# A decoder block on one core: operands of the second norm made in stages and carried into the gate projection's first group

## The chip, the cores and the metric

The kernel runs on one core of a Trainium2 chip. The metric is the device time of one execution in microseconds. TensorE does the matrix products, VectorE and ScalarE the element-wise work that may read PSUM, GpSimd element-wise work in SBUF only, and SyncE starts the transfers.

## The reference

One layer of a hybrid decoder trunk on 512 tokens with 2048 channels, in float32:

```python
h = _rms_norm(x, norm1_g[l])
proj = h @ w_in[l]
...
mix = jnp.concatenate([out_a.astype(x.dtype), out_b.astype(x.dtype),
                       out_c.astype(x.dtype)], axis=-1)
x = x + mix @ w_out[l]
h2 = _rms_norm(x, norm2_g[l])
x = x + (jax.nn.silu(h2 @ w_gate[l]) * (h2 @ w_up[l])) @ w_down[l]
```

Here out_a is a dilated attention of 8 heads, out_b a convolution module of 512 channels and out_c a windowed attention of 16 heads; mix has 2048 columns. The feed-forward part has 5632 hidden channels (44 tiles of 128).

## The kernel before

Activations are kept transposed: a tile is 128 channels by 512 tokens. Every product is made of a high and a low part: a float32 operand is copied to a rounded format (ScalarE) and the remainder is the low part (VectorE, a subtraction). All instructions stand in the order in which the program issues them; each engine works through its own queue in that order.

**The output projection** runs in two halves over the rows of mix: ROWS[0:8] and ROWS[8:16]. In each half, 16 units (one weight tile of 128 x 1024 for one output tile n, in the order OUT_ORDER[half]) take 8 x 3 matmuls each. In the first half the output is added to x (L830); in the second it is added again (L833), which gives x2, and x2 is stored to DRAM, squared and summed into ssum2 for norm 2 (L344 to L348). split_mix (L739, L740) splits a row of mix; split_rows calls it for the next three rows ahead of a matmul. Rows a0 to a3 are split as soon as their attention is done; rows b0 to b3 wait in mix until the second half asks for them. Rows b come from the convolution.

**Ticks** are a schedule written by hand: ticks.after(n, f) runs f at the n-th next tick, ticks.drain() runs all that is due. Each output unit has two ticks, in its middle and at its end. A residual stands due at the tick in the middle of the unit after its own. After two units of the second half everything due is drained and PSUM is reopened as 4 banks of products and 2 buffers called high (two banks each).

**The feed-forward products** use a seven-product scheme (Strassen's, in a variant) over halves of channels and tokens. For a pair of tiles j and j + 8 of x2, h2_of(j) scales both (L815), forms four differences of halves (L820 to L823: n1, n3, n2, n4), and splits seven 128 x 256 operands (helper operand, L808 on ScalarE and L809 on VectorE), numbered q = 5, 1, 7, 6, 2, 4, 3 in the order of use. ops[q, j] holds a high half and a low half side by side. Pair j is made when tile j + 8 has its residual.

Weights are split two units ahead: L226 and L227 while the output projection's layout of PSUM stands, then L230 (a copy into a high buffer), L231, and L232, whose second input is that copy in PSUM. Sums of weight blocks are made on GpSimd (L178) at set units.

**Gate's first group** (g = 0) has seven units, q = 5, 1, 7, 6, 2, 4, 3, each 8 + 8 matmuls at L924 over j = 0 to 7. The first two units take j = 0 to 5, then both take j = 6 and 7 (EARLY = 6). Between them stands norm 2: norm2a sums ssum2 over channels with TensorE (L289) and takes the power on GpSimd (L356), norm2b spreads the result over partitions by transposes (L295) and copies it out (L887, L888). Both use the bank outs[3], which unit 6 needs.

Of the kernel before, what the change touches and what calls it, by code (L numbers as in the profile page):

```python
# [15 lines left out]
P = 128  # L16
T = 512
# [11 lines left out]
TAPS = 31  # L29
NB = 4  # L30

OUT_ORDER = (list(range(16)), [n + o for n in range(8) for o in (0, 8)])
TAP_TICKS = 1.72


# [78 lines left out]
def kernel(ctx: ExitStack, tc: tile.TileContext, xT, wi, wo, wgu, wd, cst_in, outT):  # L114
# [19 lines left out]
    def slot(name, dt=F32, cols=T):  # L134
        return sp.tile([P, cols], dt, name=name, tag="s")
# [146 lines left out]
    def col(i):  # L282
        return cst[:, i:i + 1]
# [7 lines left out]
    def spread(src4, name, b=None):  # L291

        b = bank(name) if b is None else b
        for i in range(NT):
            nc.tensor.transpose(b[:, i * P:(i + 1) * P], src4[:, i:i + 1].to_broadcast([P, P]), ident)  # L295
        return b
# [45 lines left out]
    def add_square(acc, x, k, tag, eng=nc.gpsimd):  # L342
        if k == 0:
            nc.scalar.activation(acc, x, AF.Square)  # L344
        else:
            sq = slot(f"{tag}{k}")
            nc.scalar.activation(sq, x, AF.Square)  # L347
            eng.tensor_add(acc, acc, sq)  # L348

    def token_scale(acc, n, name, b=None):  # L350

        b = bank(name, NT) if b is None else b
        stat_rows(b[:, :, None], acc, ones)
        v, r = small(name + "v"), small(name + "r")
        nc.vector.tensor_scalar(v, b, 1.0 / n, EPS, op0=ALU.mult, op1=ALU.add)
        nc.gpsimd.tensor_tensor(r, v, nhalf[:, :NT], op=ALU.pow)  # L356
        return v, r
# [377 lines left out]
    def split_mix(name):  # L735
        if name not in m_hi:
            m = mix.pop(name)
            hi, lo = slot(f"mh_{name}", F32R), slot(f"ml_{name}", F32R)
            nc.scalar.copy(hi, m)  # L739
            nc.vector.tensor_sub(lo, m, hi.bitcast(F32))  # L740
            m_hi[name], m_lo[name] = hi, lo
# [50 lines left out]
    def load_x(i):  # L792
        if i < KT:
            n = OUT_ORDER[0][i]
            xr[n] = slot(f"xr{n}")
            nc.sync.dma_start(xr[n], xT[n])
# [5 lines left out]
    def halves(t):  # L802
        return t[:, :TH], t[:, TH:]

    def operand(q, j, src):
        t = ops[q, j] = slot(f"h{q}_{j}", F32R)
        hi, lo = halves(t)
        nc.scalar.copy(hi, src)  # L808
        nc.vector.tensor_sub(lo, src, hi.bitcast(F32))  # L809

    def h2_of(j):
        h = []
        for n in (j, j + NJ):
            t = slot(f"h2_{n}")
            nc.scalar.activation(t, x2.pop(n), AF.Copy, scale=col(C_G2 + n))  # L815
            h.append(t)
        (h11, h12), (h21, h22) = halves(h[0]), halves(h[1])
        ta, tb = slot(f"ta{j}"), slot(f"tb{j}")
        (n1, n3), (n2, n4) = halves(ta), halves(tb)
        nc.vector.tensor_sub(n1, h11, h12)  # L820
        nc.vector.tensor_sub(n3, h12, h22)  # L821
        nc.vector.tensor_sub(n2, n3, h11)  # L822
        nc.vector.tensor_add(n4, n2, h21)  # L823
        for q, src in ((5, n1), (1, h11), (7, n3), (6, n2), (2, h21), (4, n4), (3, h22)):
            operand(q, j, src)

    def residual(n, b, half):
        if half == 0:
            t = x2[n] = xr.pop(n)
            nc.vector.tensor_add(t, t, b)  # L830
            return
        t = x2[n]
        nc.vector.tensor_add(t, t, b)  # L833
        nc.sync.dma_start(x2d[n], t)
        add_square(ssum2, t, n, "sr")
        if n >= NJ:
            h2_of(n - NJ)

    def split_rows(k):
        for name in ROWS[k:k + 3]:  # L840
# [6 lines left out]
    for half in range(2):  # L847
        for i, n in enumerate(OUT_ORDER[half]):
            if half == 1 and i == 2:
                ticks.drain()  # L850
                b = None
                open_banks(banks=4, high=2)
            b = bank(f"o{half}_{n}")
            wh, wl = next_unit()
            for kk in range(8):
                k = 8 * half + kk
                row = ROWS[k]
                while row not in m_hi and row not in mix:
                    ticks.tick()
                split_rows(k)  # L860
                s = slice(kk * P, (kk + 1) * P)
                mm3(b, wh[:, s], wl[:, s], m_hi[row], m_lo[row], kk == 0, kk == 7)
                if kk % 4 == 3 or i == 0:
                    ticks.tick()
            ticks.after(0, residual, n, b, half)
            if half == 0:
                load_x(i + 2)
        for row in ROWS[8 * half:8 * half + 8]:
            if half == 0:
                m_hi.pop(row), m_lo.pop(row)  # L870
    ticks.drain()
    m_hi = m_lo = r1b = mult_a = bias_a = bias_c = None


# [5 lines left out]
    outs = [bank(f"out{i}") for i in range(4)]  # L880

    def norm2a():
        n2["r"] = token_scale(ssum2, D, "n2", outs[3][:, :NT])[1]

    def norm2b():
        b = spread(n2["r"], "r2s", outs[3])
        nc.scalar.copy(R_12, b)  # L887
        nc.scalar.copy(r2b[:, T:], b[:, :TH])  # L888

# [188 lines left out]
            at = LAID.index(q)  # L1078
            nc.sync.dma_start(acts[q, j].bitcast(F32), od[j % NP][:, at * T:(at + 1) * T])

    EARLY = 6
    blk = gate = None
    for g in range(2 * NP + len(DOWN)):
        t = g - 2 * NP
        if t < 0:
            p, m = GU_ORDER[g // 2], g % 2
            blk = Wide(p, m, gate if m else None)
            gate = blk if m == 0 else None
        else:
            n, first, end = DOWN[t]  # L1090
            blk = Down(t)
        early_w = []
        for i, q in enumerate(ORDER):
            sums_now()
            run(evacs)
            w = next_unit()
            if g == 0 and i < 2:
                blk.multiply(q, w, [ops[q, j] for j in range(EARLY)], last=False)
                early_w.append((q, w))
                if i == 1:  # L1100
                    for q, w in early_w:
                        blk.multiply(q, w, [ops[q, j] for j in range(EARLY, NJ)], EARLY)
                    norm2a()
            elif t < 0:
                blk.multiply(q, w, [ops[q, j] for j in range(NJ)])
            else:
                blk.multiply(q, w, [acts[q, j] for j in range(first, end)])
            if g == 0 and i == 2:
                norm2b()

            if t == -1:
                for j in range(NJ):
                    ops.pop((q, j))
                later(1, load_act, q, range(*DOWN[0][1:]), queue=extras)
            elif 0 <= t < len(DOWN) - 1:
                for j in range(first, DOWN[t + 1][1]):
                    acts.pop((q, j))
                later(1, load_act, q, range(end, DOWN[t + 1][2]), queue=extras)
            if t >= -1 and i == 3:
                load_y(t + 1)  # L1120
            run(extras)
# [85 lines left out]
```

## Time and profile before

| | |
|---|---|
| median of three runs | 1922.81 us (1922.43 to 1924.07) |
| the profiled execution | 1922.99 us |
| its span | 1921.2 us |
| mean granted TensorE clock | 0.996 |
| TensorE busy | 1893.5 us (99%) |
| VectorE, ScalarE, GpSimd busy | 75%, 69%, 60% |
| second half of the output projection | about 519 to 608 us |
| gate's first group | from 607.7 us |

A row of a timeline reads: start and length in us, engine, line, operation, output <- inputs, count; in brackets, how long the engine was idle before and which instruction ended that. PE is TensorE, PEld its weight load, DVE VectorE, ACT ScalarE, POOL GpSimd, SP SyncE. Rows of a line give minimum, median and maximum in ns, then the first and last start. In a tile's name ssum stands for ssum2 too, and h for the operands.

### The profile page before, as it was taken

The numbers are of one execution on the slowest core, as the hardware profiler recorded it, in microseconds if no ns is written. First come the engines' busy times: TensorE is split into PE (matmuls) and PEld (weight loads), VectorE is DVE, ScalarE is ACT, GpSimd is POOL, SyncE is SP. The second block draws the span as 40 slices with busy tenths as digits, with TensorE's granted clock in tenths as the row PEclk, the third lists the DMA queues.
The fourth block names the chain that finished last, engine by engine and source line by source line (L and its number), as shares of the span: only waits on it lengthen the run. The fifth ranks groups of instructions, "written<-read, shape, count | busy, mean of one in ns | idle before, by whom it ended". The sixth has DMA issues, their size and how long they took to land.

```text
span 1921.2 us, 29755 instructions
## 1 busy us (share of the span) xinstructions
PE 1893.5 (99%) x10332; PEld 1641.9 (85%) x10332; DVE 1436.5 (75%) x2436; ACT 1325.0 (69%) x1836; POOL 1143.4 (60%) x766
## 2 busy tenths in 40 slices
PE   8999999999998999999999999999999899999999
PEld 7888888878786888888888888888888788888888
DVE  6788888896467677777777777777777677767776
ACT  6355655454256788888888888888878677667675
POOL 5134423422013788878887888788877666656564
PEclk9999999999999999999999999999999999999999
DMA  7233333333342344444444544354437878777685
GB/s 265 86 124 94 88 106 98 89 95 125 115 132 66 132 160 161 141 159 162 161 149 143 176 141 172 126 178 152 165 137 276 289 277 279 257 251 267 207 273 193
DMA packets 135974, 320.29 MB, mean 167 GB/s; under 512 B 15504, under 2 KB 30992, under 8 KB 135824
## 3 DMA queue, kind: packets, MB, share of 16 engines
q1 hardware_dynamic: 135680, 318.30, 49.0%
q8 instruction: 81, 1.33, 0.3%
q14 instruction: 69, 0.57, 0.1%
q10 hardware_dynamic: 144, 0.10, 0.0%
HBM read 255.42 MB, written 55.31 MB: 162 GB/s over the span
## 4 chain that ended last, share of the span: by engine, by line
PE 69%; DVE 1%; DMA 1%; ACT 0%; issue 0%; POOL 0%; DVEq 0%; SPq 0%; POOLq 0%; ACTq 0%
PE out L924 66%; PE o L250 1%; PE o L249 1%; PE o L251 1%; DMA a<-od 1%; DMA od<-a 0%; DMA w('22', 'd1')_15107<-in_wd 0%; DVE tb L822 0%; DVE xr L833 0%; DVE h L809 0%; ACT h L815 0%; DVE ta L821 0%; DVE wl L232 0%; DVE wl L227 0%; POOL w('21', 'd1')_15105 L178 0%
## 5 line engine op out<-in xcount | busy, mean ns | idle before, releaser
L924 PE MATMUL out<-h,wh 128*128 128x512 f32 x2464 | 591.0, 392 | 5.1 <-DVE h L809 5.1
L924 PEld LDWEIGHTS out<-h,wh 128*128 128x128 f32 x2464 | 454.1, 189 | 93.2 <-DVE h L809 5.5
L924 PEld LDWEIGHTS out<-h,wl 128*128 128x128 f32 x2464 | 317.2, 192 | 16.2 <-DVE wl L232 2.8
L924 PE MATMUL out<-h,wl 128*128 128x256 f32 x2464 | 321.1, 283 | 3.5 <-DVE wl L232 2.6
L924 PE MATMUL out<-a,wh 128*128 128x512 f32 x1232 | 297.3, 392 | 4.1 <-DMA a<-od 2.8
L924 PEld LDWEIGHTS out<-a,wh 128*128 128x128 f32 x1232 | 226.0, 188 | 49.4 <-DMA a<-od 4.7
L227 DVE TENSOR_TENSOR wl<-w,wh 128x1024 fp32r<-128x1024 f32 (+1 forms) x93 | 115.0, 1238 | 93.0 <-ACT wh L226 91.2
L226 ACT CAST wh<-w 128x1024 fp32r<-128x1024 f32 (+1 forms) x93 | 96.8, 1041 | 104.4 <-PE o L250 30.5
L924 PEld LDWEIGHTS out<-a,wl 128*128 128x128 f32 x1232 | 160.4, 193 | 8.1 <-DMA a<-od 1.5
L924 PE MATMUL out<-a,wl 128*128 128x256 f32 x1232 | 163.0, 284 | 0.9 <-DMA a<-od 0.9
L937 DVE TENSOR_TENSOR y<-y,out 128x256 f32<-128x256 f32 x120 | 50.5, 421 | 63.8 <-PE out L924 61.3
L426 DVE SCALAR_TENSOR_TENSOR y<-bu,cst,y 128x511 f32<-128x511 f32 (+14 forms) x120 | 89.8, 749 | 0.6
L348 POOL TENSOR_TENSOR ssum<-ssum,sr 128x512 f32<-128x512 f32 x15 | 19.6, 1308 | 110.2 <-ACT sr L347 110.1
L938 DVE TENSOR_TENSOR y<-y,out 128x256 f32<-128x256 f32 x120 | 50.5, 421 | 4.1
L250 PE MATMUL o<-ml_c,wh 128*128 128x512 f32 x128 | 50.7, 396 | 2.5 <-DVE ml_c L740 2.5
L249 PE MATMUL o<-mh_c,wh 128*128 128x512 f32 x128 | 51.3, 401 | 0.0
L249 PE MATMUL cq<-hh,wh 128*128 128x512 f32 x128 | 51.2, 400 | 0.0
L251 PE MATMUL o<-mh_c,wl 128*128 128x512 f32 x128 | 50.5, 394 | 0.0
L251 PE MATMUL cq<-hh,wl 128*128 128x512 f32 x128 | 50.0, 391 | 0.0
L250 PE MATMUL cq<-hl,wh 128*128 128x512 f32 x128 | 49.9, 390 | 0.0
L348 POOL TENSOR_TENSOR ssum<-ssum,sq 128x512 f32<-128x512 f32 x15 | 25.1, 1672 | 22.6 <-ACT sq L347 22.1
L654 POOL TENSOR_SCALAR a3e<-a3e,a3d 128x128 f32<-128x128 f32 (+3 forms) x8 | 11.0, 1384 | 35.8 <-DVE a3d L652 29.5
(3093 smaller groups left out, 4923.3 us busy)
## 6 DMA issues: line engine op xcount, KB each, us to landing
a<-od SPq DMA_DIRECT2D x182, 256.0 KB, 5.4
od<-a SPq DMA_DIRECT2D x147, 256.0 KB, 3.4
w<-in_wi SPq DMA_DIRECT2D x59, 512.0 KB, 3.7
w<-in_wo SPq DMA_DIRECT2D x32, 512.0 KB, 3.6
y<-x2d SPq DMA_DIRECT2D x48, 256.0 KB, 5.4
x2d<-y SPq DMA_DIRECT2D x64, 128.0 KB, 3.3
x<-in_xT SPq DMA_DIRECT2D x16, 256.0 KB, 7.2
xr<-in_xT SPq DMA_DIRECT2D x16, 256.0 KB, 3.8
```

Source lines behind the costliest of these rows:

```text
L226: nc.scalar.copy(hi[:, :n], t[:, :n])
L227: eng.tensor_sub(lo[:, :n], t[:, :n], hi[:, :n].bitcast(F32))
L249: nc.tensor.matmul(out, wh, xh, start=start, stop=False)
L250: nc.tensor.matmul(out, wh, xl, start=False, stop=False)
L251: nc.tensor.matmul(out, wl, xh, start=False, stop=stop)
L348: eng.tensor_add(acc, acc, sq)
L426: nc.vector.scalar_tensor_tensor(yconv[j][:, i:], hconv[j][:, :T - i], c, yconv[j][:, i:], op0=ALU.mult, op1=ALU.add)
L654: nc.gpsimd.tensor_scalar(e[:, o:o + n], e[:, o:o + n], rd[:, i:i + 1], None, op0=ALU.mult)
L924: nc.tensor.matmul(out, lhs[:, s], rhs, start=begin, stop=last and low == flip[0] and x is xs[-1], skip_group_check=True)
L937: sign(out, out if first is None else first, main)
L938: sign(out, out, rest)
```

## The change

h2_of is taken apart into stages. residual now runs right behind its unit. One stage, scale_x2, is due at the next tick: scaling and square on ScalarE. add_x2 is due one tick later: for tiles 0 to 7 the difference n1, for tiles 8 to 15 the differences n3, n2 and n4, on GpSimd, and for tile 15 on VectorE; the square's sum follows one tick later on the same engine. The operands are split one tick after the differences, and operands 4 and 3 another tick later. Operands 1 and 5 of pair j need only tile j, and so are made before tile j + 8 is there.

The last four tiles of the second half are 6, 7, 14, 15 instead of 6, 14, 7, 15. What is still due when the output projection ends is not drained but run at ticks inside gate's first two units, which are cut into halves j = 0 to 3 and j = 4 to 7. The parameter EARLY is gone. Norm 2 moves one unit back (behind units 7 and 6) and takes a high buffer instead of outs[3]. Rows of the second half are split behind units 8 to 15 of the first half.

```diff
-OUT_ORDER = (list(range(16)), [n + o for n in range(8) for o in (0, 8)])
+OUT_ORDER = (list(range(16)), [n + o for n in range(6) for o in (0, 8)] + [6, 7, 14, 15])
...
-    def h2_of(j):
-        h = []
-        for n in (j, j + NJ):
-            t = slot(f"h2_{n}")
-            nc.scalar.activation(t, x2.pop(n), AF.Copy, scale=col(C_G2 + n))
-            h.append(t)
-        (h11, h12), (h21, h22) = halves(h[0]), halves(h[1])
-        ta, tb = slot(f"ta{j}"), slot(f"tb{j}")
-        (n1, n3), (n2, n4) = halves(ta), halves(tb)
-        nc.vector.tensor_sub(n1, h11, h12)
-        nc.vector.tensor_sub(n3, h12, h22)
-        nc.vector.tensor_sub(n2, n3, h11)
-        nc.vector.tensor_add(n4, n2, h21)
-        for q, src in ((5, n1), (1, h11), (7, n3), (6, n2), (2, h21), (4, n4), (3, h22)):
-            operand(q, j, src)
+    h2, tops = {}, {}
...
         nc.sync.dma_start(x2d[n], t)
-        add_square(ssum2, t, n, "sr")
-        if n >= NJ:
-            h2_of(n - NJ)
+        ticks.after(0, scale_x2, n)
+
+    def scale_x2(n):
+        t = x2.pop(n)
+        h2[n], sq = slot(f"h2_{n}"), slot(f"sr{n}")
+        nc.scalar.activation(h2[n], t, AF.Copy, scale=col(C_G2 + n))
+        nc.scalar.activation(sq if n else ssum2, t, AF.Square)
+        ticks.after(1, add_x2, n, sq)
+
+    def add_x2(n, sq):
+        j = n % NJ
+        eng = nc.gpsimd if n < KT - 1 else nc.vector
+        if n < NJ:
+            tops[j] = slot(f"ta{j}")
+            (h11, h12), n1 = halves(h2[j]), tops[j][:, :TH]
+            eng.tensor_sub(n1, h11, h12)
+            ticks.after(1, operands, j, (1, h11), (5, n1))
+        else:
+            (h11, h12), (h21, h22) = halves(h2.pop(j)), halves(h2.pop(n))
+            ta, tb = tops.pop(j), slot(f"tb{j}")
+            n3, (n2, n4) = ta[:, TH:], halves(tb)
+            eng.tensor_sub(n3, h12, h22)
+            eng.tensor_sub(n2, n3, h11)
+            eng.tensor_add(n4, n2, h21)
+            ticks.after(1, operands, j, (7, n3), (6, n2), (2, h21))
+            ticks.after(2, operands, j, (4, n4), (3, h22))
+        if n:
+            ticks.after(1, eng.tensor_add, ssum2, ssum2, sq)
...
-            ticks.after(0, residual, n, b, half)
+            residual(n, b, half)
             if half == 0:
                 load_x(i + 2)
+                if i >= 8 and ROWS[i] in mix:
+                    split_mix(ROWS[i])
...
-    ticks.drain()
     m_hi = m_lo = r1b = mult_a = bias_a = bias_c = None
...
     def norm2a():
-        n2["r"] = token_scale(ssum2, D, "n2", outs[3][:, :NT])[1]
+        n2["b"] = psum["high"].tile([P, 1024], F32, name="n2s", tag="h")
+        n2["r"] = token_scale(ssum2, D, "n2", n2["b"][:, :NT])[1]
...
-            if g == 0 and i < 2:
-                blk.multiply(q, w, [ops[q, j] for j in range(EARLY)], last=False)
-                early_w.append((q, w))
-                if i == 1:
-                    for q, w in early_w:
-                        blk.multiply(q, w, [ops[q, j] for j in range(EARLY, NJ)], EARLY)
-                    norm2a()
+            if g == 0 and ticks.due:
+                for first in (0, NJ // 2):
+                    blk.multiply(q, w, [ops[q, j] for j in range(first, first + NJ // 2)], first, first > 0)
+                    ticks.tick()
...
-            if g == 0 and i == 2:
-                norm2b()
+            if g == 0 and i in (2, 3):
+                (norm2a, norm2b)[i - 2]()
```

More of the change, by code (lines that the diff above doesn't have):

```diff
@@ L834, in residual, with operands @@
         nc.sync.dma_start(x2d[n], t)
-        add_square(ssum2, t, n, "sr")
-        if n >= NJ:
-            h2_of(n - NJ)
+        ticks.after(0, scale_x2, n)
[24 more added lines that the diff above has]
+            ticks.after(1, eng.tensor_add, ssum2, ssum2, sq)
+    def operands(j, *made):
+        for q, src in made:
+            operand(q, j, src)
     def split_rows(k):
@@ L882, in norm2a @@
     def norm2a():
-        n2["r"] = token_scale(ssum2, D, "n2", outs[3][:, :NT])[1]
+        n2["b"] = psum["high"].tile([P, 1024], F32, name="n2s", tag="h")
+        n2["r"] = token_scale(ssum2, D, "n2", n2["b"][:, :NT])[1]
     def norm2b():
-        b = spread(n2["r"], "r2s", outs[3])
+        b = spread(n2["r"], "r2s", n2.pop("b")[:, T:])
         nc.scalar.copy(R_12, b)
@@ L1079, in load_act @@
             nc.sync.dma_start(acts[q, j].bitcast(F32), od[j % NP][:, at * T:(at + 1) * T])
-    EARLY = 6
     blk = gate = None
@@ L1091 @@
             blk = Down(t)
-        early_w = []
         for i, q in enumerate(ORDER):
```

## The prediction

> **What bounds the kernel now.** I read the page first, then the waits of TensorE, the chain of waits and the windows around the one place where TensorE stands still, then the timeline there.
>
> ```profile
> PE 1893.5 (99%) x10332; PEld 1641.9 (85%) x10332; DVE 1436.5 (75%) x2436; ACT 1325.0 (69%) x1836; POOL 1143.4 (60%) x766
> ```
>
> TensorE is the bound: 27.7 of 1921.2 us lie outside its busy time. The change can only win where TensorE waits, or runs slowly, so the next view is its waits from 500 to 740 us (total, times, longest).
>
> ```profile
> PE out L924 <- DVE h L809: 5.1, 1, 5.1
> PE out L924 <- DVE wl L232: 2.6, 1, 2.6
> PE o L250 <- DVE ml_b L740: 1.1, 2, 0.9
> PE out L924 <- ACT r2b L888: 0.9, 1, 0.9
> PE o L249 <- DVE xr L833: 0.8, 1, 0.8
> ```
>
> Four of the five stand in what the change touches: L809 makes operands, L740 splits a row of the second half, L888 evacuates norm 2, and L232 (a weight's low part) was queued behind operands on VectorE. The fifth, L833, is the reopening of PSUM, which stays. The chain of waits (start, length, what):
>
> ```profile
> 612.48 1.21 DVE xr L833 x2
> ...
> 615.60 1.27 DVE ta L821
> 616.89 2.46 DVE tb L822
> ...
> 620.19 2.50 PE out L924 x7
> ...
> 624.19 4.93 PE out L924 x16
> ...
> 630.51 109.51 PE out L924 x627
> ```
>
> The last two residuals go through scaling, four differences and seven splits in one piece before gate's first product can end. The gap also costs clock (window, its length, TensorE's busy time, granted clock, DMA):
>
> ```profile
> 610.00:612.50 2.50, 0.00 (x0) 1.00 0.00 0
> 615.20:617.00 1.80, 0.00 (x0) 1.00 0.07 25
> 618.00:619.00 1.00, 0.00 (x0) 0.63 0.00 0
> 619.00:620.20 1.20, 0.01 (x1) 0.50 0.00 0
> 628.00:629.00 1.00, 1.00 (x9) 0.75 0.74 303
> ```
>
> 2.5 us of idleness left the clock at 1.00; in the second gap it fell about 3.1 us after the last matmul (the mean 0.63 puts it at 618.3), and it came back only at 628.5, over 8 us after work returned. The Trainium skill, "TensorE: Matmul & The Clock Gate", section "HAM oscillation", asks for no idle gap over about 3.4 us; the trace has 3.1. By the page's figure the rival in which the clock falls would set in 0.3 us later, and the forecast's stall stay clear of it.
>
> **The change part by part.** *First, the end of the output projection.* What it costs now, on TensorE:
>
> ```profile
> 607.71 1.52 PE L924 MATMUL out<-h,wh 128*128 128x512 f32 x6
> 631.57 3.82 PE L924 MATMUL out<-h,wh 128*128 128x512 f32 x16
> 690.89 2.08 PE L924 MATMUL out<-h,wl 128*128 128x256 f32 x16
> 696.46 2.08 PE L924 MATMUL out<-h,wl 128*128 128x256 f32 x16
> L289 PE MATMUL n<-ones,ssum x8: 164/250/250, 51.8 to 52.5; 128*128 128x1 f32 x8
> L295 PE MATMUL r1s<-ident,n1r x4: 271/272/273, 55.4 to 55.8; 128*128 128x128 f32 x4
> ```
>
> The output projection ends at 607.71 (call it 0). The 16 matmuls at 631.57 are the second half of unit 6 and the first of unit 2, so gate's fifth unit begins at 631.57 + 8 x 0.23 = 633.4, 25.7 us after 0. In the steady state two units take 696.46 - 690.89 = 5.57 us, 2.79 each. Four units are 11.15; norm 2's sums at full clock, by norm 1's row, 52.5 - 51.8 + 0.25, about 1.0; the four transposes 0.6. That is 12.75 us. So at most 25.7 - 12.75 = **12.95 us** can go.
>
> Whether they go depends on the last residual's way into operands. Units 5 and 1 need only first halves (tiles 6 and 7, added two and three units before the end) until 5.57 us; unit 7 is the first to need tile 15. The work moved to GpSimd meets VectorE on the way:
>
> ```profile
> 616.54 2.52 POOL L178 TENSOR_TENSOR w('s', 'g1')_5687<-w('s', 'g1')_5687,w('11', 'g1')_5554 128x1024 f32<-128x1024 f32 x1
> 619.38 0.42 DVE L823 TENSOR_TENSOR tb<-tb,h 128x256 f32<-128x256 f32 x1
> 686.25 2.43 POOL L178 TENSOR_TENSOR w('s', 'u2')_6432<-w('s', 'u2')_6432,w('12', 'u2')_6412 128x1024 f32<-128x1024 f32 x1 [0.98 <-ACT u1n L999]
> 687.34 1.22 DVE L232 TENSOR_TENSOR wl<-w('12', 'u2')_6412,wn 128x1024 fp32r<-128x1024 f32 x1 [0.17 <-DMA w('22', 'g3')_6571<-in_wgu]
> 702.74 0.74 POOL L987 TENSOR_TENSOR u2ta<-u2r,u2l 128x256 f32<-128x256 f32 x1
> 21.93 3.47 DVE L339 SCALAR_TENSOR_TENSOR hl<-x,cst,hh 128x512 fp32r<-128x512 f32 x2
> 23.23 1.62 POOL L348 TENSOR_TENSOR ssum<-ssum,sq 128x512 f32<-128x512 f32 x1
> ```
>
> L822, a 0.42 us difference by L823's row, took 2.46 us (chain, above) because it stood from 616.89 until GpSimd's sum of 616.54 was over. L232, one of whose inputs is in PSUM, kept its 1.22 us beside the sum at 686.25. So a VectorE operation with both inputs in SBUF and a GpSimd sum exclude each other. The rows at 21.93 and 23.23 show a second thing: between two VectorE operations that were both ready, GpSimd's next one got in. A difference costs 0.74 us on GpSimd against 0.42.
>
> The Trainium skill speaks against such a move: "Perfetto Trace Analysis", section "Optimizing Scalar/DVE Operations", says that shifting work between VectorE and GpSimd may not help, because they share a read port. By that rule the slower rival below would be the likely case, and the time 1928 instead of 1910.5; the trace bears the exclusion out, and the next sum is whether there is room for it.
>
> ```profile
> L348 POOL TENSOR_TENSOR ssum<-ssum,sr x15: 1287/1293/1478, 532.2 to 615.2; 128x512 f32<-128x512 f32 x15
> L833 DVE TENSOR_TENSOR xr<-xr,o x16: 673/680/686, 527.3 to 613.0; 128x512 f32<-128x512 f32 x16
> 523.67 0.39 PE L249 MATMUL o<-mh_a,wh 128*128 128x512 f32 x1
> 529.11 0.39 PE L249 MATMUL o<-mh_a,wh 128*128 128x512 f32 x1
> 601.19 0.68 DVE L833 TENSOR_TENSOR xr<-xr,o 128x512 f32<-128x512 f32 x1
> 620.39 0.42 DVE L809 TENSOR_TENSOR h<-ta,h 128x256 fp32r<-128x256 f32 x1
> 621.73 0.42 DVE L809 TENSOR_TENSOR h<-h,h 128x256 fp32r<-128x256 f32 x1
> ```
>
> An output unit is 529.11 - 523.67 = 5.44 us (the same place in two units). Per pair of units (10.9 us) the two engines now need, exclusively: GpSimd 4 x 0.74 + 2 x 1.29 = 5.5; VectorE two weight splits (1.22 each, by L232's row) and seven operands at (621.73 - 620.39)/4 = 0.335, 4.8. Together 10.3 of 10.9: tight, but it fits, and the residuals (0.68, from PSUM) run beside GpSimd. Today VectorE falls far behind: the fourth unit from the end is over at 607.71 - 3 x 5.44 = 591.4, its residual ran at 601.19, behind the operands in one piece. Cut into stages, each wait is at most one GpSimd operation. The two weight sums in the fourth and third units from the end (2.5 each) push VectorE some 2 us back; gate's first two splits read PSUM and let it catch up, so I take tile 15's residual as on time.
>
> From 0, VectorE: residual 0.7, split of gate's third weight to 1.9. Tile 14's residual runs at -5.4; with ScalarE's weight copy and scaling in between (some 2.3 us) and three differences (2.2), GpSimd is free at about -1.0. It runs its weight sum to 1.45 and tile 14's square sum to 2.75, which VectorE must let pass. Then five operands of pair 6 (1.7) and tile 15's three differences (1.3, kept on VectorE): 5.75. The fourth weight's split stands before the operands in the queue: 6.9. Operand 7 of pair 7: 7.25. TensorE wants it at 5.57 + 7 x 0.23 = 7.2: no stall worth a number. The fourth split also frees GpSimd's next weight sum (L178, 2.4 us), which asks when operand 7 is in work and, as at 23.23, gets in before operand 6: to 9.65. Then two operands and tile 15's square sum on VectorE (0.68): 11.0. Norm 2's sums wait for that; unit 7 ended at 8.4. So a new stall of **2.6 us** in front of norm 2, short of the 3.1 that cost the clock. Behind the waiting TensorE stand unit 6 and all gate; weights and evacuations have their time meanwhile. The power on GpSimd is ready by 14.7, unit 6 ends at 14.8, so the transposes wait for nothing; norm 2 in its own PSUM tile removes the 0.9 us on L888 (within the 12.95). This part: 12.95 - 2.6 = **10.35 us**.
>
> The bounds of that stall are 0.4 us (GpSimd does not get in: square sum at 8.65) and some 5 us, plus clock, if VectorE enters the stage 2 to 3 us late.
>
> *Second, the split rows.*
>
> ```profile
> 518.67 0.39 PE L251 MATMUL o<-mh_a,wl 128*128 128x512 f32 x1
> 520.53 0.50 PE L250 MATMUL o<-ml_b,wh 128*128 128x512 f32 x1 [0.85 <-DVE ml_b L740]
> 522.53 0.40 PE L250 MATMUL o<-ml_b,wh 128*128 128x512 f32 x1
> ```
>
> From 518.67 to 522.53 there are eight matmul steps of 0.227 us (5.44 / 24), 1.8 us; they took 3.86. The four split pairs move two to five units forward (11 to 27 us), one behind each of units 10 to 13. Gain **2.0 us**; bounds 1.1 (the waits listed) and 2.0. If their cover were gone they would cost just that.
>
> *Third, edits with one answer.* Residuals queue directly behind their unit, ahead of the next weight split and, on SP's queue, their store ahead of the next weight load. Both the residual and that split wait for the same end of a unit, so the residual fills the split's wait: 0. The halves of units 5 and 1 issue the same matmuls: 0. The second half's drain behind two units remains, and with it L833's 0.8 us.
>
> Sum: 10.35 + 2.0 = 12.35 us. The profiled execution took 1922.99 us (span 1921.2), 0.18 above the median of 1922.81, so the forecast is 1922.81 - 12.35 = **1910.5 us**.
>
> **The rivals.** *TensorE runs through* (GpSimd does not get in): 2.2 us better, 1908.3. For it: only one row pair shows the getting in. *The stall passes 3.1 us and the clock falls*: VectorE enters the gate up to 3 us late. That adds 0.7 to 3 us of stall and about 10 us (618.3 to 628.5) at half clock, 5 us: 1916 to 1918.5. Against it: gate's first two splits don't need the shared side. *Slower: exclusion during the second half.* If VectorE in fact waits for every GpSimd operation in full, its own work per pair (4.8 + 2 x 0.68) and GpSimd's 5.5 come to 11.7 of 10.9 us, plus some 0.1 for each of half a dozen hand-overs (the sum at 616.54 took 2.52 against 2.43): 12.3, so 1.4 behind per pair, 10 over seven pairs, 15 with the two weight sums. Operand 7 of pair 7 is then 15 us late, with 5 us for the clock: 12.75 + 20 = 32.8 against 25.7, 7.1 worse, less 2.0 for the rows: 1928. It decides from about 12 us of lateness on. Against it: GpSimd's operations come when VectorE waits for TensorE or ScalarE anyway. *Given back*: what follows gate's first group is short of weights or operands and the gain is lost there: 1921 to 1923. Against it: after 630.51 the chain runs on TensorE alone for 109.51 us.
>
> **How the numbers follow.** Forecast 0.52, runs through 0.20, clock falls 0.15, slower 0.08, given back 0.05. About 0.2% (3.8 us) is what a measurement can tell here. The first three are faster by more: 0.87; same 0.05; slower 0.08. The range goes from running through with the rest of the kernel 1 us either way, 1907.0, to the middle of the clock's case, 1917.0.
>
> **What would show it.** Right: the first-half split shows no wait on L740; TensorE goes from the last output unit into unit 5 without a gap; one wait of 2 to 3 us stands at L289, ended by VectorE's last square sum, with GpSimd's L178 beside it; the granted clock stays at 1.00; differences show at 0.74 us on GpSimd. Wrong: a granted clock under 1.00 behind the output projection, residuals more than 5 us late in the second half, or a wait for operand 7.

## The result and the profile after

The kernel after takes **1913.38 us** (1912.56 to 1914.18 in four runs) beside 1923.44 us (1922.43 to 1924.35 in four) for the kernel before: ratio 0.9948, 95% interval 0.9931 to 0.9965. That is faster by 10.1 us; the forecast was 12.35 us faster. Its profiled execution took 1913.02 us (span 1911.2). The page's row of engines:

```profile
PE 1889.6 (99%) x10332; PEld 1639.4 (86%) x10332; DVE 1441.7 (75%) x2408; ACT 1323.7 (69%) x1836; POOL 1165.1 (61%) x794
```

TensorE is outside its busy time for 21.6 us, 6.1 less than before. The rest of the 10 us is not visible here, because a TensorE at half clock counts as busy. Next, the waits of TensorE from 500 to 740 us (total, times, longest):

```profile
PE n2s L289 <- DVE ssum L94: 2.0, 1, 2.0
PE out L941 <- DVE h L809: 0.9, 1, 0.9
PE o L249 <- DVE xr L819: 0.9, 1, 0.9
```

Three are left of five, and the last is the reopening of PSUM that was to stay. The wait on L740 is gone. The square sums are issued by the tick helper, so they stand under its line 94. TensorE's timeline gives the places (start, length, what, idle time before it in brackets):

```profile
518.72 0.39 PE L249 MATMUL o<-mh_b,wh 128*128 128x512 f32 x1
...
605.55 1.07 PE L941 MATMUL out<-h,wh 128*128 128x512 f32 x4
...
613.82 0.50 PE L941 MATMUL out<-h,wh 128*128 128x512 f32 x1 [0.93 <-DVE h L809]
...
617.28 1.05 PE L289 MATMUL n2s<-ones,ssum 128*128 128x1 f32 x8 [2.01 <-DVE ssum L94]
...
623.00 2.10 PE L941 MATMUL out<-h,wh 128*128 128x512 f32 x8
```

Gate's first product starts at 605.55 instead of 607.71, 2.16 us sooner. The split rows make 2.0 of that: from the first product with a row b (518.72) to gate's first product it is 86.83 us, where the kernel before takes 607.71 - 519.18 = 88.53, and 0.3 us are saved just ahead of that row. From 605.55 to gate's fifth unit at 623.00 it is 17.45 us, instead of 25.7: 8.25 us. Together 10.4, against 10.0 between the two spans. The forecast for the second distance was 12.75 + 2.6 = 15.35; the excess over 12.75 is 4.7 us. Of it 0.93 is a wait for operand 7 of pair 7 and 2.01 the wait in front of norm 2. The remainder is in the windows (window, length, TensorE's busy time, granted clock, DMA):

```profile
619.00:619.50 0.50, 0.50 (x5) 0.80 0.00 0
622.50:623.00 0.50, 0.50 (x6) 0.79 0.59 221
```

A mean of 0.80 over half a microsecond means that 0.2 us of it were at 0.5: the clock fell at 619.30, and by the second row it rose at 622.71. So 3.41 us ran at half clock, which costs 1.7 us. 0.93 + 2.01 + 1.7 = 4.64, nearly the whole excess. Why operand 7 was late, on VectorE:

```profile
600.50 1.51 DVE L809 TENSOR_TENSOR h<-ta,h 128x256 fp32r<-128x256 f32 x1
601.93 0.67 DVE L819 TENSOR_TENSOR xr<-xr,o 128x512 f32<-128x512 f32 x1
...
605.75 0.69 DVE L819 TENSOR_TENSOR xr<-xr,o 128x512 f32<-128x512 f32 x1 [0.41 <-PE o L251]
...
607.49 1.11 DVE L809 TENSOR_TENSOR h<-ta,h 128x256 fp32r<-128x256 f32 x1
608.52 1.51 DVE L809 TENSOR_TENSOR h<-tb,h 128x256 fp32r<-128x256 f32 x1
...
613.35 0.42 DVE L809 TENSOR_TENSOR h<-ta,h 128x256 fp32r<-128x256 f32 x1
613.68 2.60 DVE L809 TENSOR_TENSOR h<-tb,h 128x256 fp32r<-128x256 f32 x1
...
616.54 0.68 DVE L94 TENSOR_TENSOR ssum<-ssum,sr 128x512 f32<-128x512 f32 x1
```

and on GpSimd:

```profile
605.14 0.80 POOL L844 TENSOR_TENSOR tb<-tb,h 128x256 f32<-128x256 f32 x1
605.91 2.41 POOL L178 TENSOR_TENSOR w('s', 'g1')_5693<-w('s', 'g1')_5693,w('11', 'g1')_5541 128x1024 f32<-128x1024 f32 x1
608.28 1.47 POOL L94 TENSOR_TENSOR ssum<-ssum,sr 128x512 f32<-128x512 f32 x1
...
613.56 2.44 POOL L178 TENSOR_TENSOR w('s', 'g1')_5693<-w('s', 'g1')_5693,w('12', 'g1')_5642 128x1024 f32<-128x1024 f32 x1 [3.81 <-ACT h L808]
```

Tile 14's residual started at 601.93, 3.6 us before the end of the output projection at 605.55 (5.4 in the forecast): it stood behind the operand of 600.50, which took 1.51 us instead of 0.42 beside a square sum on GpSimd (600.25, 1.48 us). So its differences ended on GpSimd at 605.94 and not at 604.55. The weight sum and square sum behind them ran to 609.75, and two operands of VectorE beside them took 1.11 and 1.51 us instead of 0.42. Later, between operands 7 and 6, GpSimd's weight sum of 613.56 got in, although VectorE's next operation was ready: that operation shows 2.60 us. This is the getting in that the forecast had built its 2.6 us stall on.

### The profile page after: what moved, and what is told of

Read it like the earlier page. It is cut to its first block, busy times and chain, and to the rows that moved or that the text cites. A ratio compares the mean times of both kernels' runs of the same rounds, so it can differ in the third digit from the quotient of the medians.

```text
span 1911.2 us, 29738 instructions
## 1 busy us (share of the span) xinstructions
PE 1889.6 (99%) x10332; PEld 1639.4 (86%) x10332; DVE 1441.7 (75%) x2408; ACT 1323.7 (69%) x1836; POOL 1165.1 (61%) x794
## 4 chain that ended last, share of the span: by engine, by line
PE 96%; DMA 2%; DVE 1%; POOL 1%; issue 0%; SPq 0%; ACT 0%; POOLq 0%; ACTq 0%; DVEq 0%
PE out L941 66%; PE o L249 3%; PE o L251 3%; PE o L250 3%; PE cq L249 2%; PE cq L251 2%; PE cq L250 2%; PE ak L249 1%; PE ak L251 1%; PE ak L250 1%; PE av L251 1%; PE av L249 1%; PE av L250 1%; PE aq L249 1%; PE aq L250 1%; PE aq L251 1%
## 5 line engine op out<-in xcount | busy, mean ns | idle before, releaser
L836 POOL TENSOR_TENSOR ta<-h 128x256 f32<-128x256 f32 x8 | 7.3, 908 | 58.5 <-issue 44.9
```

Source lines behind the costliest of these rows:

```text
L836: eng.tensor_sub(n1, h11, h12)
```

## The experiments

The theory: the gain is the 2 us of rows plus 12.75 against 25.7 us in gate's first group, less two waits and a piece of half clock, each of which an edit can take away. The rivals: GpSimd itself carries the gain; or the order of tiles does; or the drain does. Times are medians, in five rounds against the kernel before: 1923.22 us (15 runs) for the first four, 1922.77 (8) for the next four, 1924.18 (9) for the last three. Kernels of different groups are compared by how far each lies below its own group's kernel before. The intervals reach some 2.5 us to either side; where two edits lie closer than that, the times do not tell them apart, and the traces, one execution each, have to.

**The kernel after again.**

> The changed kernel once more, beside the three below on the same chip. Theory A (the gain is 2.1 us from the rows and 8.3 us from the end, cut by three things in gate's first group: 0.9 us for operand 7, 2.0 us for the square sum behind a GpSimd weight sum, and 1.8 us at half clock): 10 us below the kernel before. The two waits have set causes in the queues, so they return with 0.9 and 2.0 us within 0.2. On the clock: if it falls at the borders of a window of fixed length that runs on its own, the fall comes at another place or not at all in this execution, and the part of the 4.7 us that is half clock differs by up to 2 us; if it falls a fixed time after TensorE's last matmul, it comes again about 4.1 us after 615.3 and costs 1.8.

1914.16 us, ratio 0.9953 (0.9941 to 0.9966). The same two waits (2.0 and 0.94) and again one piece of 3.41 us at half clock; 17.45 us from gate's first product to its fifth unit. The division above is repeatable. The clock fell at the same place (619.22), which by the expectation speaks for a fixed time behind the last matmul; the edits below and the account of the clock further down show that it is not.

**The rows alone**: the kernel before with the early split.

```diff
             if half == 0:
                 load_x(i + 2)
+                if i >= 8 and ROWS[i] in mix:
+                    split_mix(ROWS[i])
```

> The kernel before with the early split of the second half's rows alone. Theory A: the wait on L740 in the second half's first unit goes and nothing takes its place: 2.1 us below the kernel before (1.5 to 2.5), gate's stage as before with 25.7 us from the last output unit to gate's fifth. Rival B (what is won ahead of the end is given back there, because VectorE and GpSimd set the pace at the end): TensorE reaches gate 2 us sooner, the operands do not, and the kernel is within 0.5 us of before.

1920.72 us, ratio 0.9988 (0.9979 to 0.9997): 2.5 us faster. From the first product with row b to gate's first product:

```profile
519.07 0.39 PE L249 MATMUL o<-mh_b,wh 128*128 128x512 f32 x1
...
605.90 1.52 PE L926 MATMUL out<-h,wh 128*128 128x512 f32 x6
```

86.83 us, where the kernel before takes 607.71 - 519.18 = 88.53:

```profile
519.18 0.49 PE L249 MATMUL o<-mh_b,wh 128*128 128x512 f32 x1
```

With 0.3 us saved ahead of that row (519.18 - 518.67 = 0.51, where a step is 0.23), this is the 2.0 us. Gate's stage is as it was, as expected: the 16 matmuls of this row are the second half of unit 6 and the first of unit 2, so the fifth unit begins at 629.39 + 8 x 0.23 = 631.2, 25.3 us behind 605.90.

```profile
629.39 3.82 PE L926 MATMUL out<-h,wh 128*128 128x512 f32 x16
```

**The change without the rows.**

```diff
-                if i >= 8 and ROWS[i] in mix:
-                    split_mix(ROWS[i])
```

> The changed kernel without the early split of rows. Theory A: 2.1 us slower than the changed kernel, so 7.5 to 8.5 below the kernel before, with the same waits in gate's first group. Rival B: within 0.5 us of the changed kernel, with gate's waits 2 us shorter.

1915.46 us, ratio 0.9962 (0.9949 to 0.9974): only 1.3 us above the repeat of the kernel after, where 2.1 were expected. The first product with a row b, gate's first product, and the clock in gate's stage:

```profile
517.69 0.50 PE L249 MATMUL o<-mh_b,wh 128*128 128x512 f32 x1
...
605.68 1.07 PE L939 MATMUL out<-h,wh 128*128 128x512 f32 x4
```

```profile
617.00:618.00 1.00, 0.59 (x3) 0.70 0.00 0
624.00:625.00 1.00, 1.00 (x7) 0.88 0.00 0
```

87.99 us against 86.83 for the kernel after, 1.2 us, and 0.3 ahead of it: in this kernel the rows are worth 1.4 us in the profile, somewhat less than in the kernel before. The gate stage holds the same waits as the kernel after (2.0 and 0.9), but here the clock was at half from 617.40 to 624.24, 6.84 us: 3.4 us lost by the same waits that cost 1.7 above. That is a first sign that the length of a wait does not decide. The 1.4 us of the rows and the 1.7 of the clock make more than the 1.3 us between the times and the 1.8 between the two spans (1913.2 and 1911.4): in this execution the output projection had begun 0.8 us sooner than in the kernel after (410.04 and 410.87), ahead of all that the edit touches. So the rows' worth inside the change is not known to better than about a microsecond.

**One tick earlier.** A third tick behind gate's first unit brings the last operands ahead of the fourth weight's split.

```diff
                 for first in (0, NJ // 2):
                     blk.multiply(q, w, [...], first, first > 0)
                     ticks.tick()
+                if i == 0:
+                    ticks.tick()
```

> The changed kernel with one more tick behind gate's first unit: operands 7, 6 and 2 of the last pair and tile 15's square sum are issued ahead of the fourth weight split instead of behind it; nothing else. Theory A (the waits come from the order in the queues): operand 7 is ready before TensorE wants it, the square sum is done when unit 7 ends since the GpSimd weight sum that got in can start only after the fourth split, both waits fall under 0.3 us, the clock stays at 1.00 in gate's first group, and the time from the last output unit to gate's fifth goes from 17.5 to about 13: 4 us below the changed kernel (3 to 4.7). Rival B (the shared side of VectorE and GpSimd is full in this stage): the wait moves to the fourth weight split (L232) with 2 to 3 us, and the kernel stays within 1 us of the changed one.

1909.78 us, ratio 0.9933 (0.9920 to 0.9945). Waits, and VectorE:

```profile
PE n2s L289 <- DVE wl L232: 0.9, 1, 0.9
```

```profile
613.56 0.69 DVE L94 TENSOR_TENSOR ssum<-ssum,sr 128x512 f32<-128x512 f32 x1
614.16 1.21 DVE L232 TENSOR_TENSOR wl<-w('s', 'g1')_5693,wn 128x1024 fp32r<-128x1024 f32 x1
```

The square sum is done by 614.25 instead of 617.22: both waits and the fall of the clock are gone. What is late next is the high buffer that norm 2 takes: the fourth weight's split holds it until 615.37. That is the wait of the expectation's rival B, with 0.94 us instead of 2 to 3. Gate's stage takes 13.87 us, and the kernel lies 4.4 us below the repeat, where 4 were expected.

**The last weight sum one unit later**, so that it cannot get in (the sum of block 12, for gate's first group only).

```diff
-        sums[u + 2].append(add("s", "s", "12"))
+        g1 = name == "g1"
+        sums[u + 2 + g1].append(add("s", "s", "12", "12" if g1 else None))
...
-            ("12", True), ...
+            ("12", not g1), ...
```

> The changed kernel with one GpSimd instruction later: in gate's first group the weight sum that got in between operands 7 and 6 of the last pair (L178, third sum of the group) is issued one unit later, behind tile 15's square sum. Theory A (that sum makes the 2.0 us in front of norm 2, and the fall of the clock follows from the wait): the wait at L289 falls under 0.3 us, the 0.9 us for operand 7 stays, the clock stays at 1.00, 3 to 4 us below the changed kernel. Rival B (VectorE has too much to do here, whoever gets in): the wait at L289 stays at 1 us or more.

1909.35 us, ratio 0.9930 (0.9916 to 0.9944). The wait in front of norm 2 is gone, the other stays:

```profile
PE out L942 <- DVE h L810: 0.9, 1, 0.9
```

```profile
615.00:617.00 2.00, 2.00 (x16) 0.78 0.00 0
619.00:621.00 2.00, 2.00 (x11) 0.87 0.03 8
```

So the weight sum is what made the 2.0 us. But the clock fell here too, from 616.12 to 619.52, behind a wait of 0.94 us and the eight matmuls of one column for norm 2. That went against the expectation. The stage, 15.23 us, is 2.2 us shorter than the repeat's, while the kernel lies 4.4 us further below the kernel before than the repeat does (13.4 against 9.1). The profiled execution, 1910.57 us, is the slowest of the five; the clocks of the others inside the stage are not known.

**Everything on VectorE.**

```diff
-        eng = nc.gpsimd if n < KT - 1 else nc.vector
+        eng = nc.vector
```

> The changed kernel with all differences and square sums on VectorE, none on GpSimd. Theory A says that the stages give the gain, not GpSimd: per pair of output units VectorE then has two residuals, two splits, seven operands, four differences and two sums, some 8.9 of 10.9 us, with no GpSimd instruction beside it but the weight sums; operand 7 comes up to 0.9 us sooner, the weight sum still gets in before norm 2's sums: 0 to 1.5 us below the changed kernel. Rival D (GpSimd carries the gain): VectorE falls behind again and the kernel is 3 us or more above the changed one. The Trainium skill's rule on moving work between these two engines (Perfetto Trace Analysis, Optimizing Scalar/DVE Operations) would have it no slower either; no number of the above comes from it.

1910.45 us (1909.67 to 1913.67), ratio 0.9940 (0.9926 to 0.9954): 12.3 us below the kernel before, where the repeat of the kernel after lies 9.1 below. That is no slower than with GpSimd: the loss of rival D did not come, and the gain is larger than theory A's 0 to 1.5 us.

```profile
PE n2s L289 <- DVE ssum L94: 2.0, 1, 2.0
```

```profile
613.00:617.00 4.00, 1.99 (x17) 1.00 0.01 2
617.00:621.00 4.00, 4.00 (x24) 1.00 0.39 106
```

Operand 7 is on time, the weight sum still gets in (2.0 us), and this wait, without the one of 0.93 us ahead of it, costs no clock at all.

**The old order of the last tiles** (6, 14, 7, 15).

```diff
-OUT_ORDER = (..., [n + o for n in range(6) for o in (0, 8)] + [6, 7, 14, 15])
+OUT_ORDER = (..., [n + o for n in range(8) for o in (0, 8)])
```

> The changed kernel with the old order of the last tiles (6, 14, 7, 15). Operands 1 and 5 of pair 7 are then split inside gate's first unit, while those of pair 6 are all done before. Theory A: TensorE waits 0 to 1.5 us for operand 5 in gate's first unit, but VectorE has five operands less to make between the last residual and the last pair, so operand 7 comes before it is wanted and the square sum about as unit 7 ends: the waits of 0.9 and 2.0 us go, and the kernel is between 2 us below and 1 us above the changed one. Rival E (the order is what lets gate start at once): a wait of 3 us or more in unit 5 and the clock falling, 4 us or more above the changed kernel.

1912.96 us, ratio 0.9945 (0.9932 to 0.9958), no different from the kernel after. The two waits are replaced by another, with the clock at half for 3.41 us behind it:

```profile
PE out L941 <- DVE h L809: 2.9, 1, 2.9
```

```profile
611.61 1.95 PE L941 MATMUL out<-h,wh 128*128 128x512 f32 x5 [2.92 <-DVE h L809]
```

```profile
605.10 2.62 DVE L809 TENSOR_TENSOR h<-tb,h 128x256 fp32r<-128x256 f32 x1
607.65 1.50 DVE L809 TENSOR_TENSOR h<-h,h 128x256 fp32r<-128x256 f32 x1
609.08 0.67 DVE L819 TENSOR_TENSOR xr<-xr,o 128x512 f32<-128x512 f32 x1
```

Here a weight sum, and behind it a square sum, get in ahead of tile 15's residual, which runs at 609.08, and operand 5 of pair 7 is split only behind it. The wait stands in gate's first unit, behind 15 of its 16 matmuls, and is twice as long as theory A's 0 to 1.5 us. The third weight sum gets in as before (an operand of 2.62 us at 614.19), but TensorE is late enough not to wait for it. The order moves the meeting of the two engines; it does not remove it.

**The second weight sum sooner as well** (on top of the earlier tick, the sum of block 11 goes one unit ahead).

```diff
-        sums[u].append(add("s", "s", "11", "11"))
+        sums[u - g1].append(add("s", "s", "11", None if g1 else "11"))
...
-            ("11", False), ...
+            ("11", g1), ...
```

> The kernel with one more tick behind gate's first unit (e4), and besides the second weight sum of gate's first group one unit sooner, ahead of tile 14's differences on GpSimd: it then runs before the last residual instead of beside the operands of pair 6. In e4 TensorE still waited 0.9 us at norm 2 for the fourth weight split, which follows the square sum on VectorE. Theory A: VectorE loses some 2 us less to GpSimd, that wait goes, the clock stays at 1.00, and the time from the last output unit to gate's fifth is 12.8 to 13.2: 0.5 to 1.2 us below e4, so about 14 us below the kernel before. Rival B: the sum delays tile 14's differences and so the operands of pair 6, and the kernel is no faster than e4.

1909.29 us, ratio 0.9930 (0.9917 to 0.9943): nothing on top of the earlier tick (13.5 us below the kernel before, against 13.4). The operands came sooner, but the third weight sum came sooner too:

```profile
PE n2s L296 <- POOL n2r L357: 1.8, 1, 1.8
```

```profile
612.57 2.61 DVE L810 TENSOR_TENSOR h<-h,h 128x256 fp32r<-128x256 f32 x1
...
616.83 0.15 DVE L356 TENSOR_SCALAR n2v<-n2s 128x4 f32<-128x4 f32 x1
```

It got in again, now ahead of norm 2's evacuation (616.83), so the power and then the transposes came late by 1.8 us.

**The drain back**: what is due is run in one piece behind the output projection.

```diff
+    ticks.drain()
     m_hi = m_lo = r1b = mult_a = bias_a = bias_c = None
```

> The changed kernel with the drain put back behind the output projection: the stages are kept, but all that is due runs ahead of gate's first unit, so the last pair's operands stand in front of the third weight's split instead of between gate's units. Theory A (carrying the stages into gate is what keeps the weight splits on time): operand 7 and the square sum are early, and TensorE waits some 3.6 us for the third weight's low part (L232) in front of unit 7 instead; 16.3 us from the last output unit to gate's fifth plus one or two clock windows (1.7 or 3.4 us): 0.5 to 2.5 us above the changed kernel. Rival F (carrying does nothing, the stages alone gain): within 0.5 us of the changed kernel, no wait on L232.

1914.54 us, ratio 0.9950 (0.9937 to 0.9962).

```profile
PE out L942 <- ACT wh L231: 3.9, 1, 3.9
```

```profile
614.43 1.22 DVE L232 TENSOR_TENSOR wl<-w('21', 'g1')_5438,wn 128x1024 fp32r<-128x1024 f32 x1
```

Gate's third weight is split behind all the operands, 8 us later than in the kernel after (606.36), and gate's third unit waits 3.9 us for its high part from ScalarE (L231), which is as late. The other waits are gone; the stage takes 18.1 us with one piece at half clock, against 17.45. So carrying the stages into gate's units, as the change does, was worth only some 0.7 us of the stage over the drain as long as the weight sums stayed where they are, and nothing that the times show (0.9950 against 0.9948 and 0.9953).

**All three edits together** (earlier tick, second sum sooner, third sum later), with GpSimd as in the change, and with everything on VectorE.

> The three moves together: one more tick behind gate's first unit (e4), the second weight sum one unit sooner (e8) and the third one unit later (e5). In e8 the 0.9 us for the split went, but the third sum got in ahead of norm 2's evacuation on VectorE, and the transposes waited 1.8 us for the power. Theory A: that wait goes too, nothing is left between the output projection and gate's fifth unit beyond 0.3 us, the clock stays: 12.8 to 13.1 us there, some 1.5 us below e4, e5 and e8, 14.5 us below the kernel before (13.5 to 15.5). Rival B (each wait removed lets in another as long): within 0.7 us of e4, e5 and e8.

> The same three moves with all differences and square sums on VectorE. Theory A: VectorE has the time without GpSimd's help, so nothing differs on TensorE: within 0.7 us of the kernel with the three moves. Rival D (GpSimd carries something after all): 1 us or more above it.

1908.80 us (1907.18 to 1909.40), ratio 0.9919 (0.9906 to 0.9933), and 1908.21 us (1907.87 to 1908.70), ratio 0.9917 (0.9904 to 0.9931). The first of them:

```profile
PE o L250 <- DVE xr L820: 0.9, 1, 0.9
```

```profile
605.71 1.07 PE L942 MATMUL out<-h,wh 128*128 128x512 f32 x4
...
618.42 2.09 PE L942 MATMUL out<-h,wh 128*128 128x512 f32 x8
```

No wait is left from 500 to 740 us but the reopening of PSUM, and gate's stage takes 12.71 us. The second takes 12.49. Both are faster than the kernel before and than the kernel after: 15.4 and 16.0 us below the kernel before, against 10.1 and 9.1. From the single edits (13.4 to 13.5) the times do not separate them; the waits and the stage do. In the first of them the second weight sum still gets in once (an operand of 2.62 us at 600.67), but 5 us ahead of gate, where nothing waits for it. With the meetings out of TensorE's way, no difference can be seen between the two engines for the differences and square sums.

The stages side by side, each from gate's first product to its fifth unit; the sum is 12.75 plus the waits plus half of the time that TensorE worked at half clock (in the kernel before and with the rows alone it also stood still at half clock, for 1.9 and 4.2 us, which the waits already hold):

| kernel | stage, us | waits | working at half clock | sum |
|---|---|---|---|---|
| before | 25.7 | 2.6 + 5.1 + 0.9 | 8.3 | 25.5 |
| rows alone | 25.3 | 2.6 + 4.2 + 0.9 | 9.4 | 25.2 |
| after | 17.45 | 0.93 + 2.01 | 3.41 | 17.4 |
| after again | 17.45 | 0.94 + 2.0 | 3.41 | 17.4 |
| without the rows | 19.0 | 0.9 + 2.0 | 6.84 | 19.1 |
| tick earlier | 13.87 | 0.94 | 0 | 13.7 |
| last sum later | 15.23 | 0.94 | 3.41 | 15.4 |
| all on VectorE | 14.68 | 2.0 | 0 | 14.8 |
| old order | 17.2 | 2.9 | 3.41 | 17.4 |
| second sum sooner | 14.7 | 1.8 | 0 | 14.6 |
| drain | 18.1 | 3.9 | 3.41 | 18.4 |
| all three | 12.71 | 0 | 0 | 12.75 |
| all three, on VectorE | 12.49 | 0 | 0 | 12.75 |

## Why the prediction was right, and where it was not

**The mechanism held in the main.** Besides the rows, the gain lay where the prediction put it: in TensorE's standing still between the output projection and gate's fifth unit, and in the clock that this costs. The 12.75 us that it would need without a stall is what the three edits together reached (12.71 and 12.49). In the kernel before, tile 15's residual ran at 613.0, 5.3 us behind the end of the output projection; now it runs 0.2 behind. Which part of the change does that is shown only by elimination: the engine, the order of tiles and the carrying past the drain were each undone, and most of the gain stayed. The stages themselves, the residuals right behind their units and norm 2's own bank were not undone one by one, so that the stages carry the gain is argued and not shown. Of the three signs of being wrong that the prediction named, two were seen: a granted clock under 1.00, and a wait for operand 7.

**The rows**: 2.0 us forecast, 2.0 in the second half of the change's profile (88.53 - 86.83 + 0.3) and in that of the rows alone; 2.5 alone in the times, with an interval from 0.6 to 4.0.

**The getting in**: forecast, and shown. One weight sum between operands 7 and 6 held VectorE for 2.60 us, the wait in front of norm 2 was 2.0 instead of 2.6, and moving that sum alone removed it. It is shorter because TensorE had already lost 0.93 us to operand 7; what norm 2's sums wait for, the square sum, came 0.7 us later than forecast (617.22 - 605.55 = 11.7 instead of 11.0). The rival in which TensorE runs through therefore did not come about, though the edited versions got to its time.

**Operand 7 of pair 7** was to be no stall worth a number; it was 0.93 us. The mis-sized term is the start of tile 14's residual, 3.6 us before the end of the output projection and not 5.4, and what followed from it: GpSimd free at +0.4 and not at -1.0, so that its two long operations fell onto VectorE's operands. Tile 15's residual was on time, as taken (605.75, 0.2 behind the end).

**The step that failed is the clock.** From "2.5 us of idleness left the clock at 1.00" and a fall 3.1 us into the second gap, the prediction took 3.1 us as a threshold and kept its stall of 2.6 clear of it. The clock fell 4.0 us after TensorE had stopped at 615.27, with TensorE at work again since 617.28; without the rows it fell 2.0 us after the stop, behind the same two waits, and with everything on VectorE, behind a wait of 2.0 us, not at all. So no fixed time behind the last matmul decides. In one experiment it fell behind a wait of 0.94. The rival in which the clock falls came true in kind, though at 1.7 us and not at 5. What decides is seen in how long it stayed down. The kernel before:

```profile
618.20:618.40 0.20, 0.00 (x0) 0.64 0.00 0
...
628.30:628.60 0.30, 0.30 (x3) 0.68 0.90 369
```

and the rows alone:

```profile
612.00:612.50 0.50, 0.50 (x3) 0.73 0.78 287
...
625.50:626.00 0.50, 0.50 (x4) 0.62 1.07 434
```

618.26 to 628.49 is 10.24 us, 612.23 to 625.88 is 13.65; with 6.84 and 3.41 above these are one, two, three and four times 3.41. Two other places show where such windows begin. In the kernel after the clock also fell behind a wait of 2.47 us for the split of a row and behind one of 2.08 us for a transfer:

```profile
417.50:418.50 1.00, 0.77 (x3) 0.71 0.71 221
1489.50:1490.00 0.50, 0.50 (x4) 0.70 0.38 141
```

That is at 417.92 and at 1489.70, and each time for 3.41 us. From 417.92 to 619.30 it is 201.38 us, 59 times 3.413; from 619.30 to 1489.70 it is 870.40, 255 times. In the kernel before, too, the fall at 618.26, from which the prediction took its 3.1 us, lies 201.39 us behind one at 416.87. In each of the thirteen profiles all falls and rises of the clock up to 1510 us lie on one such grid, to within 0.05 us. So the clock changes at the ends of windows of 3.41 us that follow one another through the whole execution, whatever TensorE does, and a wait costs 0, 1.7 or 3.4 us by what part of which window it takes. The waits of 2.01 and 0.93 us cost 1.7 in the kernel after and, with the same lengths, 3.4 without the rows; the 2.0 us that were left with everything on VectorE cost nothing. This agrees with the Trainium skill, "TensorE: Matmul & The Clock Gate", section "What's actually happening", which gives a window of about 3.4 us; the rule in its section "HAM oscillation" that the prediction cited, no gap over about 3.4 us, is not enough by these runs. Which share of a window must be busy, and whether matmuls of one column count, the runs don't settle: the clock fell behind a window in which the profile counts 2.47 us as busy, the eight matmuls of one column among them (612.69 to 616.10, last sum later), and not behind one with 1.58 (616.20 to 619.61, second sum sooner). A kernel with such a wait need not lose the same in each execution: of the five runs of all on VectorE four lie between 1909.67 and 1910.60 us and one at 1913.67; two windows more would be enough for that. Its mean granted clock, 0.996 against 0.998 in the profiled execution, would fit them, but one of the four has 0.996 too, so this stays open.

With 0.93 for operand 7 and 1.7 for the clock, less 0.6 for the smaller stall and the 0.16 by which gate began sooner than the rows alone make, the forecast's 12.35 becomes 10.5, against 10.1 measured. That the time came out 2.3 us from the forecast is in part luck: two misses of 0.93 and 1.7 us were partly offset by the smaller stall, and with the windows lying otherwise the clock would have cost 0 or 3.4.

**The slower rival**, exclusion all through the second half, needed a lateness of 12 us by the prediction, of 10 by its own terms (25.7 + 2.0 - 12.75 - 5). Tile 14's residual was 1.8 late and tile 15's not at all. Exclusion is there, but VectorE catches up: ahead of 8 of the 16 residuals it stood idle, 18.4 us in all, until TensorE had finished the unit. **Given back** did not come about: gate's fifth unit comes 10.4 us earlier and the span is 10.0 shorter.

**GpSimd's part.** The prediction weighed the Trainium skill's warning, "Perfetto Trace Analysis", section "Optimizing Scalar/DVE Operations", that moving work between these two engines may not help, and let the exclusive sum of 10.3 in 10.9 us decide. The residuals confirmed that it fits; the runs bear the warning out as well. With everything on VectorE the change lies 12.3 us below the kernel before, against 9.1 with GpSimd's help, and its trace has no wait for operand 7; with the three edits the two variants are the same within the noise (1908.21 and 1908.80). So the engine does not make the gain. The tick of the last operands and the places of two weight sums make what the change left over, 4.7 us of the stage.

## What to carry to other kernels

Where two engines exclude each other, look for each long operation of the one and ask which short one of the other stands behind it just then; moving one such operation by one unit took a wait of 2.0 us away here, while giving 43 short ones from VectorE to GpSimd gained nothing, and with the sums in their old places cost a wait of 0.93 us. Price a wait of TensorE with the clock as a chance (nothing, or half of one window or two), not as a threshold on its length. And judge an edit by the waits that are left behind it: the old order, the drain and the sooner sum each removed one wait and raised another of 1.8 to 3.9 us.

## What the hardware showed that was not expected

The time at half clock was a multiple of 3.41 us wherever its end was seen. In gate's stage it was 3.41 us in five profiles, 6.84, 10.24 and 13.65 in one each, and nothing in five. At two other places it was there before and after the change: near 417 us in twelve of the thirteen profiles, with 3.41 us, and between 1482 and 1503 us in all, with 3.41 in ten and 6.83 in three. So two executions can differ by 1.7 us through places that an edit does not touch.

GpSimd's waiting operation got in between two VectorE operations in at least eight kernels, each time seen as a VectorE operation of 2.60 to 2.63 us instead of 0.42, beside a GpSimd sum of 2.44 to 2.59. Each time ScalarE's half of the operand that was passed had been made before.
